# A trunk layer with RWKV-7, S5 and a gated MLP: S5's inputs without the norm's root, S5 tables by exchanged halves, one scan per batch, and masks of block products ranked first

## The chip, the cores and the metric

The kernel runs on one core of a Trainium2 chip. The metric is the device time of one execution in microseconds (us). TensorE is called PE in the profile, VectorE DVE, ScalarE ACT, GpSimd POOL, and SyncE, which issues most transfers, SP.

## The reference

One layer, 1024 tokens by 1024 channels in float32. The input projection feeds three consumers: RWKV-7 (8 heads of 64), S5 (32 groups of 16 channels with 64 complex states each), and two gates.

```python
h = rms_norm(x, norm_mix_pre)            # x * rsqrt(mean(x*x) + 1e-6) * g
proj = h @ w_in                          # [r,k,v, low-rank downs | u_s5 | gates]
o_rwkv = rwkv7_branch(p_rwkv, ...) @ w_branch_rwkv
o_s5   = s5_branch(u_s5, ...) @ w_branch_s5
mixed = (g_rwkv * o_rwkv + g_s5 * o_s5) @ w_out
x = x + rms_norm(mixed, norm_mix_post)
x = x + rms_norm(conv_ffn(rms_norm(x, norm_ffn_pre), ...), norm_ffn_post)

def s5_branch(u, ...):
    a_bar = exp(lam * dt); b_bar = ((a_bar - 1) / lam) * b
    bu = einsum('gpc,blgc->blgp', b_bar, ug)
    states = scan(s[t] = a_bar * s[t-1] + bu[t])
    y = real(einsum('gcp,blgp->blgc', c, states)) + d * ug
    y = gelu(y); return y * sigmoid(y @ w_glu + b_glu)
```

RWKV-7 scans a 64 by 64 state per head, `S = S*w + (S a) b^T + v k^T`, with decay, removal key and in-context rate made from projections of h.

## The kernel before, in words

Activations lie transposed, channels on the partitions, in 8 tiles of 128 channels and two halves of 512 tokens (th = 0 and 1). Each fp32 matmul is three: operands are split into a rounded high part (a cast, by ACT) and the rest (a subtraction, mostly DVE), and high times high (L172), low times high (L173) and high times low (L174) are summed. `hh` and `hl` are the parts of the normed input, `wh` and `wl` (for two of S5's four weight tiles `lx`) those of a weight; `gm` and `chk` are PSUM tiles.

PE's order is written out by hand. A few *lanes* hold the dependent chains (the norm, S5's tables, S5's batches, RWKV's fronts, its chain, the outputs). A list `fill` of long products (the mixing inputs `mix_in`, the gates) is laid between the steps of the lanes. A lane's `yield` names a due time T_*, in us on a clock that counts the matmuls laid down; until then fills run. The other engines' instructions are placed by a scheduler with priorities: HPN is the highest, then HPW, HP2, HP.

The start of the program: `load_x` loads x for a half; `norm` squares it, sums over channels with `sumsq` (four one-column matmuls per pair of tiles), takes the root with `rstd` (nine small DVE steps), spreads it with one matmul per 128 tokens (`spread`, L271), multiplies x by weight and root (L969) and splits. Only then does `s5_in` multiply, 4 output tiles by 2 halves by 8 input tiles by 3 matmuls, 192 in all, and ACT moves the results out of PSUM in an 8-element stride (L1075). Half 1's norm stands between these matmuls. `s5_setup` makes small 128x32 tables, after which `mix_in` and the gates fill around S5's lanes.

Per S5 batch b (8 groups), `s5_tables` makes complex products of the input and output tables (`bb`, `bw`, `bx`, `ca`, `cb`) and a cosine and a sine table of 128x8x128 (`cs`, `sn`, L569 to L578); `s5_batch` rotates the inputs (L600 to L602), scans 8 groups (L605), rotates back (L607, L608) and multiplies with PE (L613 to L615). The time step table s["rho"] holds the moduli.

In `rwkv_front` two pairs of heads (`prep_lane(0)` and `(1)`) each make their key, decay and removal-key tiles (L669 to L706), block products on PE (`cz`, L718), and a mask that DVE applies to them (L721). The outputs go through `rwkv_out` (transposes L918), a store to YR, a load, a split, and the product `mm<-t` in `merge_rk`.

Of the kernel before, what the change touches and what calls it, by code (L numbers as in the profile page):

```python
# [13 lines left out]
ALU = mybir.AluOpType  # L14
# [52 lines left out]
class Kern:  # L67
# [207 lines left out]
    def setup(self):  # L275
        nc = self.nc
        self.vecs = self.const.tile([128, NVEC], F32, name="vecs")
        self.csts = self.const.tile([128, NCST], F32, name="csts")
        nc.gpsimd.dma_start(self.csts[:, 0:128], self.a["cst"][:, 0:128])
        nc.gpsimd.dma_start(self.vecs, self.a["vec"])  # L280
        nc.gpsimd.dma_start(self.csts[:, 128:NCST], self.a["cst"][:, 128:NCST])
# [6 lines left out]

        o, n = VEC["mu"]
# [15 lines left out]
    def s5_setup(self):  # L305
# [4 lines left out]
        with self.tc.tile_pool(name="s5tmp", bufs=1) as pool:  # L310
            def sm(n=32, dt=F32):
                return pool.tile([128, n], dt, name=self.nm("sm"))
            lr, li, ls = sm(), sm(), sm()
            nc.sync.dma_start(ls, a["s5_ls"])
            nc.sync.dma_start(lr, a["s5_a"][0])
            nc.sync.dma_start(li, a["s5_a"][1])
# [173 lines left out]
    def s5_tables(self, b, d):  # L490
# [23 lines left out]
        lin(bx, bre, bc_c(s["w4"]), bim, bc_c(s["w3"]), ALU.subtract, V)  # L514
# [19 lines left out]
        ct2 = self.s5p.tile([128, 8, 9, 16], F32, tag="ct", name=self.nm("ct"))  # L534
        tab(V, cb, cre, s["q2"], 1)
        tab(V, ct2, cim, s["q1"], 1)
        V.tensor_tensor(cb[:, :, 1:9, :], cb[:, :, 1:9, :], ct2[:, :, 1:9, :], ALU.subtract)
# [27 lines left out]
        nrow = self.cst("nrow").unsqueeze(1).to_broadcast([128, 8, 128])  # L565

        def bc_n(x):
            return x[:, g8].unsqueeze(2).to_broadcast([128, 8, 128])
        V.tensor_tensor(ph, nrow, bc_n(s["fh"]), ALU.mult)  # L569
        V.tensor_scalar(cs, ph, MAGIC, -MAGIC, ALU.add, ALU.add)  # L570
        V.tensor_tensor(ph, ph, cs, ALU.subtract)
        V.tensor_tensor(sn, nrow, bc_n(s["fl"]), ALU.mult)
# [5 lines left out]
        A.activation(cs, cs, AF.Sin, bias=self.hpi, scale=-SIN_SCALE)  # L578

        d.update(ca=ca, cb=cb, cs=cs, sn=sn, toep=toep, wT=wT)  # L580
        yield 1.8, T_TRIG

    def s5_batch(self, b, d, ys):
# [4 lines left out]
        ca, cb, cs, sn, toep, wT = (d[n] for n in ("ca", "cb", "cs", "sn", "toep", "wT"))  # L588
# [3 lines left out]
        G.memset(z[:, :, 0:1], 0.0)  # L592
        rot = self.t4(shape=(128, 8, 128))
        yield 0, T_US
# [5 lines left out]
        V.tensor_tensor(rot, p1, cs, ALU.mult)  # L600
        V.tensor_tensor(r2, p2, sn, ALU.mult)
        V.tensor_tensor(rot, rot, r2, ALU.add)  # L602
        for g in range(8):
            gg = b * 8 + g
            V.tensor_tensor_scan(z[:, g, 1:128], s["rho"][:, gg:gg + 1].to_broadcast([128, 127]),  # L605
                                 rot[:, g, 0:127], 0.0, ALU.mult, ALU.add)
# [35 lines left out]
    def rwkv_front(self, d, g, th, pt, start):  # L642
# [28 lines left out]
        for e in L:  # L671
            p, tz = e["p"], e["tz"]
            V.tensor_tensor_scan(tz, self.cst("smask"), tz, 0.0, ALU.mult, ALU.add)
            A.activation(e["bk1"], c64(e["ta"]), AF.Identity, bias=self.ka_1[:, p:p + 1], scale=self.ka_h[:, p:p + 1])
            V.tensor_tensor(e["bk1"], e["bk1"], c64(e["k"]), ALU.mult)
# [6 lines left out]
        for e in L:  # L682
            y = self.small.tile([128, 8], F32, tag="sv", name=self.nm("sv"), bufs=2)
            V.tensor_scalar(y, e["st"].rearrange("p a b -> p (a b)"), 1e-24, None, ALU.max)
            V.reciprocal(y, y)
            A.copy(c64(e["yb"]), y.unsqueeze(2).to_broadcast([128, 8, 64]))
        for e in L:
            p, tz = e["p"], e["tz"]
            G.memset(e["pe"][:, :, 0:1], 1.0)
            A.activation(e["pe"][:, :, 1:65], c64(tz), AF.Exp, scale=-0.5 * CDEC)  # L690
            A.activation(tz, tz, AF.Exp, scale=0.5 * CDEC)
            A.copy(pt[:, :, p], e["pe"][:, :, 64])
            V.scalar_tensor_tensor(e["bk0"], c64(e["ta"]), 1.0, c64(e["k"]), ALU.add, ALU.mult)
            V.scalar_tensor_tensor(e["ar0"], c64(e["k"]), self.vec("k_k", p), e["pe"][:, :, 0:64], ALU.mult, ALU.mult)
            V.scalar_tensor_tensor(e["bk0"], e["bk0"], self.vec("k_k", p), c64(tz), ALU.mult, ALU.mult)
# [5 lines left out]
        for e in L:  # L701
            r, tz = e["r"], e["tz"]
            V.scalar_tensor_tensor(e["bk0"], e["bk0"], -0.5, c64(e["kb"]), ALU.mult, ALU.mult)
            V.tensor_tensor(e["ar1"], c64(r), e["pe"][:, :, 1:65], ALU.mult)
            V.tensor_tensor(c64(r), c64(r), e["bk1"], ALU.mult)
            V.tensor_tensor(e["bk1"], e["bk1"], c64(tz), ALU.mult)  # L706
            e["v"] = ld(self.RKV[8 + e["p"]])
# [3 lines left out]
        for u, e in enumerate(L):  # L711
            bk, ar = e["bk"], e["ar"]
            for q in range(2):
# [6 lines left out]
                for h in range(2):  # L720
                    V.tensor_tensor(d["gr"][:, u, 4 * q:4 * q + 4, h], ps[h], gm, ALU.mult)  # L721
# [4 lines left out]
            if u:  # L726
                for blk in range(2):
                    for h in range(2):
                        q = 64 * h + 32 * blk
                        nc.gpsimd.dma_start(d["md"][blk].rearrange("(e h) q t -> h q e t", h=2)[h],  # L730
                                            d["gr"][q:q + 32, :, :, h, 32 * blk:32 * blk + 32].rearrange("p u c t -> p (u c) t"))
            else:
# [208 lines left out]
    def load_x(self, th, pool):  # L941
        xs = []
        for k in range(NK):
            x = pool.tile([128, 512], F32, name=self.nm("x"), tag="x", bufs=16)
            self.nc.sync.dma_start(x, self.a["x"][k * 128:k * 128 + 128, th * 512:th * 512 + 512])
            xs.append(x)
        return xs

    def norm(self, th, xs, pool):

        nc = self.nc
        ss = self.chk()[:, 0:512]
        yield 0, T_X
        for k in range(0, NK, 2):
            sq = [pool.tile([128, 512], F32, tag="sq", name=self.nm("sq"), bufs=4) for _ in range(2)]
            for i in range(2):
                nc.scalar.activation(sq[i], xs[k + i], AF.Square)
            nc.vector.tensor_tensor(sq[0], sq[0], sq[1], ALU.add)
            self.sumsq(ss, sq[0], k == 0)
            yield 0.9, 1.0  # L960
        bc = self.chk()[:, 0:512]
        y = self.rstd(ss, 1e-6, 1.0 / D)
        yield 0, T_RS
        self.spread(bc, y)
        rbc = pool.tile([128, 512], F32, tag="rbc", name=self.nm("rbc"), bufs=1)
        nc.scalar.copy(rbc, bc)
        h = []
        for k in range(NK):
            nc.vector.scalar_tensor_tensor(xs[k], xs[k], self.vec("g_mix_pre", k), rbc, ALU.mult, ALU.mult)  # L969
            h.append(self.hsplit(xs[k], k, self.hp[th], eng=nc.gpsimd if k % 2 else nc.vector))  # L970
        self.h[th] = h
        yield 1.7, 5.0
# [47 lines left out]
    def rkv(self, p):  # L1020

        for mt in (4 + p, p, 8 + p):
            def use(th, ps):
# [37 lines left out]

    def s5_in(self, pool):

        w = [self.load_w(self.a["w_in"][14 + b], pool=pool if b > 1 else None) for b in range(4)]
        for th in range(2):
            h = self.h[th]
            ps = [self.gmp() for b in range(4)]
            steps = [self.mm3_steps(ps[b], w[b], 0, [x[0] for x in h], [x[1] for x in h]) for b in range(4)]
            for k in range(NK):
                for b in range(4):  # L1070
# [882 lines left out]
```

## Time and profile before

| | |
|---|---|
| Median of 3 runs | 1545.65 us (1543.03 to 1549.22) |
| The profiled execution | 1545.26 us, span 1543.5, mean granted clock 0.974 |
| PE busy | 1455.5 us (94%), 9332 matmuls |
| DVE busy | 1084.8 us (70%) |
| ACT busy | 696.9 us (45%) |
| POOL busy | 74.0 us (5%) |

The span is what the profiler recorded; 1.8 us of the execution lie around it. Busy shares are averages over stages: the start is limited by other things than the channel sub-layer. A matmul of 512 columns can take twice as long while the granted clock is low.

### The profile page before, as it was taken

Reading aid. Unit: us, or ns where it says so; the run is one execution under the profiler, and the core shown is the slowest. Engines: PE = TensorE matmul, PEld = TensorE weight load, DVE = VectorE, ACT = ScalarE, POOL = GpSimd, SP = SyncE. Lnnn points to the kernel's source line nnn. Section 1 sums busy time; section 2 is a strip of 40 time slices with the busy share of each in tenths; the row PEclk is TensorE's granted clock in tenths of the full one; section 3 lists DMA queues with packets and bytes.
Section 4 is the critical chain, followed back from the end, with each engine's and each line's share of the span. In section 5 each row is a group of like instructions: output and inputs, shape, how many; then the busy total and the mean of one; then the engine's idle time right before and its main releaser. Section 6 shows DMA issues by size and latency. Waiting matters only on the chain.

```text
span 1543.5 us, 24191 instructions
## 1 busy us (share of the span) xinstructions
PE 1455.5 (94%) x9332; PEld 1191.3 (77%) x9332; DVE 1084.8 (70%) x1783; ACT 696.9 (45%) x1077; POOL 74.0 (5%) x126
## 2 busy tenths in 40 slices
PE   5999899999999899899898999999999999999996
PEld 4788788778777677678676888788888887888785
DVE  6898784845325748466587689777777777698777
ACT  5364442533324535436444446444444444443451
POOL 2100000001100010000100000000000000000001
PEclk9999999999999899999998999999999999999998
DMA  6164242623511475424864444322222225953632
GB/s 209 42 205 126 87 127 100 206 88 117 158 57 63 152 225 161 119 79 132 269 217 153 151 144 133 111 83 82 82 82 82 82 85 195 335 169 114 214 109 109
DMA packets 130339, 210.45 MB, mean 136 GB/s; under 512 B 37696, under 2 KB 43840, under 8 KB 130224
## 3 DMA queue, kind: packets, MB, share of 16 engines
q1 hardware_dynamic: 122480, 185.17, 37.4%
q0 software_dynamic: 6592, 21.64, 4.1%
q10 hardware_dynamic: 1152, 2.10, 0.4%
q8 instruction: 73, 1.20, 0.3%
q14 instruction: 42, 0.34, 0.1%
HBM read 153.28 MB, written 53.48 MB: 134 GB/s over the span
## 4 chain that ended last, share of the span: by engine, by line
PE 76%; DVE 10%; DMA 6%; ACT 4%; issue 3%; SPq 0%; POOL 0%; ACTq 0%; DVEq 0%; POOLq 0%
PE gm L172 9%; PE gm L173 8%; PE gm L174 8%; PE rp L1384 4%; PE d L1559 4%; PE d L1558 4%; PE rp L1385 4%; PE rp L1386 4%; PE d L1560 4%; PE mm L1384 2%; PE mm L1386 2%; PE mm L1385 2%; PE ch L172 1%; PE ch L173 1%; PE ch L174 1%
## 5 line engine op out<-in xcount | busy, mean ns | idle before, releaser
L172 PE MATMUL gm<-hh,wh 128*128 128x512 f32 x688 | 282.8, 411 | 11.1 <-DVE hl L1116 5.8
L173 PE MATMUL gm<-hl,wh 128*128 128x512 f32 x688 | 271.9, 395 | 0.2 <-DVE hl L227 0.2
L174 PE MATMUL gm<-hh,wl 128*128 128x512 f32 x656 | 258.4, 394 | 0.0
L156 ACT CAST wh<-wf 128x512 fp32r<-128x512 f32 x179 | 110.8, 620 | 225.0 <-PE gm L173 138.0
L157 DVE TENSOR_TENSOR wl<-wf,wh 128x512 fp32r<-128x512 f32 x175 | 120.2, 688 | 120.6 <-ACT wh L156 112.7
L172 PEld LDWEIGHTS gm<-hh,wh 128*128 128x128 f32 x688 | 130.8, 190 | 45.1 <-DVE hl L1116 7.5
L173 PEld LDWEIGHTS gm<-hl,wh 128*128 128x128 f32 x688 | 130.9, 190 | 25.7 <-issue 1.0
L174 PEld LDWEIGHTS gm<-hh,wl 128*128 128x128 f32 x656 | 124.9, 190 | 27.3
L1559 PE MATMUL d<-xl,wh 128*128 128x512 f32 x308 | 120.8, 392 | 3.0 <-DVE xl L227 3.0
L1558 PE MATMUL d<-xh,wh 128*128 128x512 f32 x308 | 121.1, 393 | 2.4 <-ACT xh L226 2.1
L1560 PE MATMUL d<-xh,wl 128*128 128x512 f32 x308 | 120.5, 391 | 0.0
L1384 PE MATMUL rp<-t,h 128*128 128x512 f32 x216 | 84.4, 391 | 1.4 <-ACT p L1398 1.4
L1386 PE MATMUL rp<-t,l 128*128 128x512 f32 x216 | 84.2, 390 | 0.5 <-DVE l L227 0.5
L1385 PE MATMUL rp<-t,h 128*128 128x512 f32 x216 | 84.1, 389 | 0.0
L1558 PEld LDWEIGHTS d<-xh,wh 128*128 128x128 f32 x308 | 58.2, 189 | 15.9 <-ACT xh L226 2.5
L1559 PEld LDWEIGHTS d<-xl,wh 128*128 128x128 f32 x308 | 58.2, 189 | 15.8 <-DVE xl L227 3.9
L1560 PEld LDWEIGHTS d<-xh,wl 128*128 128x128 f32 x308 | 58.2, 189 | 12.3
L226 ACT CAST h<-r 128x1024 fp32r<-128x1024 f32 x34 | 35.9, 1054 | 61.1 <-PE rp L1385 32.5
L227 DVE TENSOR_TENSOR l<-r,h 128x1024 fp32r<-128x1024 f32 x34 | 41.6, 1225 | 29.2 <-ACT h L226 27.7
L1405 DVE SCALAR_TENSOR_TENSOR y<-zv,vecs,y 128x1023 f32<-128x1023 f32 (+1 forms) x36 | 46.1, 1281 | 8.5 <-ACT y L1403 8.5
L1384 PEld LDWEIGHTS rp<-t,h 128*128 128x128 f32 x216 | 40.5, 188 | 10.8 <-ACT p L1398 2.2
L1386 PEld LDWEIGHTS rp<-t,l 128*128 128x128 f32 x216 | 40.5, 188 | 9.4 <-DVE l L227 1.0
(462 smaller groups left out, 3201.3 us busy)
## 6 DMA issues: line engine op xcount, KB each, us to landing
r<-in_w_up_dram SPq DMA_DIRECT2D x36, 512.0 KB, 3.6
wf<-in_w_in_dram SPq DMA_DIRECT2D x68, 256.0 KB, 2.9
st<-in_w_down_dram SPq DMA_DIRECT2D x55, 256.0 KB, 4.2
st<-ACT SPq DMA_DIRECT2D x44, 256.0 KB, 4.8
wf<-in_w_up_dram SPq DMA_DIRECT2D x36, 256.0 KB, 2.6
ACT<-y POOLq DMA_DIRECT2D x18, 512.0 KB, 2.9
GT<-ev SPq DMA_DIRECT2D x32, 256.0 KB, 2.4
wf<-in_w_br_dram SPq DMA_DIRECT2D x32, 256.0 KB, 3.4
```

What stands on the lines that cost most here:

```text
L156: nc.scalar.copy(h[:, :n], f[:, :n])
L157: nc.vector.tensor_tensor(l[:, :n], f[:, :n], h[:, :n].bitcast(F32), ALU.subtract)
L172: mm(ps, a, xh[k], start=k == 0, stop=False)
L173: mm(ps, a, xl[k], start=False, stop=False)
L174: mm(ps, b, xh[k], start=False, stop=k == n - 1)
L1384: mm(ps, wh[:, c], xh, start=first and k == 0, stop=False, skip_group_check=True)
L1385: mm(ps, wh[:, c], xl, start=False, stop=False, skip_group_check=True)
L1386: mm(ps, wl[:, c], xh, start=False, stop=k == 3, skip_group_check=True)
L1405: V.scalar_tensor_tensor(y[:, lag:], z[:, 0:1024 - lag], self.vec(nme, i), y[:, lag:], ALU.mult, ALU.add)
L1558: mm(ps, wh[:, c], xh[:, x], start=start, stop=False, skip_group_check=True)
L1559: mm(ps, wh[:, c], xl[:, x], start=False, stop=False, skip_group_check=True)
L1560: mm(ps, wl[:, c], xh[:, x], start=False, stop=stop, skip_group_check=True)
```

## The change

- **Start.** `load_x`, `norm` and `s5_in` become one function, `start`. S5's matmuls take `gained` inputs, x times the norm's weight, without the root; DVE multiplies by the root when it moves the results out of PSUM (`evict`). Squares are summed on DVE, so that one `sumsq` per half is left. The normed input for the other products is made later by `scaled`. The weights for three S5 tiles load into the tiles of `u8`. The vectors and S5's raw inputs load on ACT's queue; the rest of the constants load last on SP's.
- **S5 tables.** `bx` and `cb` are exchanged halves of `bw` and `ca`, copied by ACT. The products with the row numbers are 16 ACT activations. Eight scans of 127 become one of 1024, whose factors are copied to `ph` and whose first column in each group is zero.
- **RWKV front.** Decay exponentials come earlier, the reciprocal norm carries the factor -0.5, products are reordered, masks of the block products are ranked under HPW, and the second pair's front begins after the first pair's masks (`grams`) and after all mixing inputs (`all_in`).
- **Numbers.** T_TAB0 20 to 44, T_BK 5 to 4, T_X gone; S5's lane has priority HP2 instead of HP.

```diff
-    def norm(self, th, xs, pool):
-        ss = self.chk()[:, 0:512]
-        yield 0, T_X
-        for k in range(0, NK, 2):
-            sq = [pool.tile([128, 512], F32, tag="sq", ...) for _ in range(2)]
-            for i in range(2):
-                nc.scalar.activation(sq[i], xs[k + i], AF.Square)
-            nc.vector.tensor_tensor(sq[0], sq[0], sq[1], ALU.add)
-            self.sumsq(ss, sq[0], k == 0)
...
-            nc.vector.scalar_tensor_tensor(xs[k], xs[k], self.vec("g_mix_pre", k), rbc, ALU.mult, ALU.mult)
-            h.append(self.hsplit(xs[k], k, self.hp[th], eng=nc.gpsimd if k % 2 else nc.vector))
...
-                self.nc.scalar.copy(y.rearrange("p i n -> p n i"), ps[b].rearrange("p (n j) -> p n j", j=8)[:, :, ::-1])
+    def start(self, pool):
...
+        def gained(th, k):
+            hi, lo = self.pair(th, k)
+            g = self.vec("g_mix_pre", k)
+            A.activation(hi, xs[th][k], AF.Identity, scale=g)
+            V.scalar_tensor_tensor(lo, xs[th][k], g, hi.bitcast(F32), ALU.mult, ALU.subtract)
+            return hi, lo
+        def square(th, k):
...
+            A.activation(sq, xs[th][k], AF.Square)
+            if k % 2:
+                V.tensor_tensor(sq, sq, last[th], ALU.add)
+                if acc[th] is not None:
+                    V.tensor_tensor(sq, sq, acc[th], ALU.add)
...
+        def scaled(th, k):
+            x = xs[th][k]
+            V.scalar_tensor_tensor(x, x, self.vec("g_mix_pre", k), rbc[th], ALU.mult, ALU.mult)
+            self.h[th][k] = self.hsplit(x, k, self.hp[th], eng=V)
+        def evict(th, b, ps):
+            y = self.ev((128, 8, 64))
+            p, r = [x.rearrange("p (n j) -> p n j", j=8)[:, :, ::-1] for x in (ps, rbc[th])]
+            V.tensor_tensor(y.rearrange("p i n -> p n i"), p, r, ALU.mult)
...
+        for th in range(2):
+            ps = [self.gmp() for b in range(4)]
+            for k in range(NK):
+                for b in range(4):
...
+                    nc.tensor.matmul(ps[b], a, hi, start=k == 0, stop=False)
+                    nc.tensor.matmul(ps[b], a, lo, start=False, stop=False)
+                    nc.tensor.matmul(ps[b], l, hi, start=False, stop=k == NK - 1)
+                    if k == NK - 1:
+                        evict(th, b, ps[b])
+                if k == (1 if th else 4):
+                    y = root(th)
+                if k == (3 if th else 6):
+                    rbc[th] = scales(th, y)
+                if th:
+                    scaled(0, k)
+                elif k >= 4:
+                    for q in (2 * k - 8, 2 * k - 7):
+                        g[1].append(gained(1, q))
+                        square(1, q)
+        for k in range(NK):
+            scaled(1, k)
...
-        lin(bx, bre, bc_c(s["w4"]), bim, bc_c(s["w3"]), ALU.subtract, V)
+        A.mul(bx[HALF[0]], bw[HALF[1]], -1.0)
+        A.copy(bx[HALF[1]], bw[HALF[0]])
...
-        tab(V, cb, cre, s["q2"], 1)
-        tab(V, ct2, cim, s["q1"], 1)
-        V.tensor_tensor(cb[:, :, 1:9, :], cb[:, :, 1:9, :], ct2[:, :, 1:9, :], ALU.subtract)
+        A.copy(cb[HALF[0], :, 1:9, :], ca[HALF[1], :, 1:9, :])
+        A.mul(cb[HALF[1], :, 1:9, :], ca[HALF[0], :, 1:9, :], -1.0)
...
-        V.tensor_tensor(ph, nrow, bc_n(s["fh"]), ALU.mult)
+        for t, f in ((ph, s["fh"]), (sn, s["fl"])):
+            for g in range(8):
+                A.activation(t[:, g], self.cst("nrow"), AF.Identity, scale=f[:, b * 8 + g:b * 8 + g + 1])
...
-        V.tensor_tensor(sn, nrow, bc_n(s["fl"]), ALU.mult)
...
+        A.copy(ph, s["rho"][:, g8].unsqueeze(2).to_broadcast([128, 8, 128]))
+        G.memset(ph[:, :, 0:1], 0.0)
...
-        for g in range(8):
-            gg = b * 8 + g
-            V.tensor_tensor_scan(z[:, g, 1:128], s["rho"][:, gg:gg + 1].to_broadcast([128, 127]),
-                                 rot[:, g, 0:127], 0.0, ALU.mult, ALU.add)
+        V.tensor_tensor_scan(*(t.rearrange("p g n -> p (g n)") for t in (z, ph, rot)), 0.0, ALU.mult, ALU.add)
...
-                for h in range(2):
-                    V.tensor_tensor(d["gr"][:, u, 4 * q:4 * q + 4, h], ps[h], gm, ALU.mult)
+                with self.tc.high_priority(HPW):
+                    for h in range(2):
+                        V.tensor_tensor(d["gr"][:, u, 4 * q:4 * q + 4, h], ps[h], gm, ALU.mult)
...
-                self.drive([(HP, self.s5_lane()), (HP, self.tab_lane())])
+                self.drive([(HP2, self.s5_lane()), (HP, self.tab_lane())])
...
-T_US, T_TAB0, T_TAB, T_TRIG, T_SCAN = 5.0, 20.0, 20.0, 12.0, 13.0
+T_US, T_TAB0, T_TAB, T_TRIG, T_SCAN = 5.0, 44.0, 20.0, 12.0, 13.0
```

PE's first instructions before. `sq` are the squares, `rsy` the root, `hh` and `hl` the high and low part of an input tile:

```order
L245 MATMUL chk_241<-ones_205,sq_242 128x1 x4
L245 MATMUL chk_241<-ones_205,sq_251 128x1 x4
L245 MATMUL chk_241<-ones_205,sq_260 128x1 x4
L245 MATMUL chk_241<-ones_205,sq_269 128x1 x4
L271 MATMUL chk_278<-csts,rsy_281 128x128 x4
L172 MATMUL gm_403<-hh_299,wh_355 128x512
L173 MATMUL gm_403<-hl_300,wh_355 128x512
```

And after, the program's first matmuls, and below the "..." the place of the one sum of squares of half 0:

```order
L1037 MATMUL gm_346<-hh_259,wh_263 128x512
L1038 MATMUL gm_346<-hl_260,wh_263 128x512
L1039 MATMUL gm_346<-hh_259,wl_264 128x512
L1037 MATMUL gm_347<-hh_259,wh_267 128x512
L1038 MATMUL gm_347<-hl_260,wh_267 128x512
...
L1039 MATMUL gm_349<-hh_302,lx_319 128x512
L245 MATMUL chk_257<-ones_192,sq_342 128x1 x4
L1037 MATMUL gm_346<-hh_324,wh_306 128x512
```

The products have moved ahead of the sum and the root; the sum stands after the fifth of eight input tiles.

DVE at the program's start before: seven small operations on the vectors, then weight splits and sums of squares (`sq`, L958):

```order
L302 TENSOR_SCALAR ka_222<-vecs 128x4
L157 TENSOR_TENSOR wl_356<-wf_357,wh_355 128x512
L157 TENSOR_TENSOR wl_362<-wf_363,wh_361 128x512
L958 TENSOR_TENSOR sq_242<-sq_242,sq_243 128x512
L958 TENSOR_TENSOR sq_251<-sq_251,sq_252 128x512
```

After, the same seven, then 18 operations of `s5_setup` (`sm`), of which the last four are shown, then the first low half of an input (`hl`, L970) and the weight splits:

```order
L335 SCALAR_TENSOR_TENSOR sm_785<-sm_783,sm_779 128x32
L330 TENSOR_TENSOR sm_901<-sm_897,sm_899 128x32
L335 SCALAR_TENSOR_TENSOR sm_787<-sm_785,sm_779 128x32
L408 RECIPROCAL sm_903<-sm_901 128x32
L970 SCALAR_TENSOR_TENSOR hl_260<-x_198,vecs,hh_259 128x512
L227 TENSOR_TENSOR wl_264<-u_0_177,wh_263 128x512
L227 TENSOR_TENSOR wl_268<-u_1_178,wh_267 128x512
```

The small S5 operations have moved from the end of the input products to ahead of the first input tile's low half.

DVE in RWKV's first front before. `gr` are the masked block products (L721), `cz` their PSUM tiles; the other rows make the second pair's tiles:

```order
L721 TENSOR_TENSOR gr_2593<-cz_2827,csts 128x4x128
L705 TENSOR_TENSOR ld_2954<-ld_2954,bk_591_2868 128x512
L721 TENSOR_TENSOR gr_2593<-cz_2828,csts 128x4x128
L706 TENSOR_TENSOR bk_591_2868<-bk_591_2868,ld_2876 128x8x64
L695 SCALAR_TENSOR_TENSOR bk_591_2868<-bk_591_2868,vecs,ld_2876 128x8x64
L157 TENSOR_TENSOR wl_3151<-wf_3152,wh_3150 128x512
L704 TENSOR_TENSOR ar_2867<-ld_2957,gr_2869 128x8x64
L693 SCALAR_TENSOR_TENSOR bk_591_2868<-ld_2882,ld_2874 128x8x64
L705 TENSOR_TENSOR ld_2957<-ld_2957,bk_591_2868 128x512
L695 SCALAR_TENSOR_TENSOR bk_591_2868<-bk_591_2868,vecs,ld_2878 128x8x64
L706 TENSOR_TENSOR bk_591_2868<-bk_591_2868,ld_2878 128x8x64
L721 TENSOR_TENSOR gr_2593<-cz_2902,csts 128x4x128
```

And after (the mask is at L719 now):

```order
L703 SCALAR_TENSOR_TENSOR bk_573_2788<-bk_573_2788,vecs,rp_2982 128x8x64
L671 SCALAR_TENSOR_TENSOR ld_3060<-csts,ld_3060 128x512
L671 SCALAR_TENSOR_TENSOR ld_3062<-csts,ld_3062 128x512
L690 SCALAR_TENSOR_TENSOR ar_3051<-ld_3056,vecs,gr_3053 128x8x64
L719 TENSOR_TENSOR gr_2789<-cz_3011,csts 128x4x128
L719 TENSOR_TENSOR gr_2789<-cz_3012,csts 128x4x128
L676 TENSOR_TENSOR bk_618_3052<-bk_618_3052,ld_3056 128x8x64
L719 TENSOR_TENSOR gr_2789<-cz_3031,csts 128x4x128
L719 TENSOR_TENSOR gr_2789<-cz_3032,csts 128x4x128
```

The masks of the first pair no longer stand among the last operations of the second pair's tiles. Elsewhere in PE's order the steps of S5's lane and of RWKV's fronts stand later among the fill matmuls: the first batch's tables after 387 large matmuls instead of 285, the first front after 906 instead of 810; between the last output transposes (half 1, L918) and the first `mm<-t` there are 106 large matmuls instead of 178.

181 lines of the change are left out of this document (99 added, 82 removed).

## The prediction

> **What bounds the kernel now.** I read the page first, then busy time by stretch, then TensorE's and the other engines' timelines at the places that the change touches.
>
> ```profile
> span 1543.5 us, 24191 instructions
> PE 76%; DVE 10%; DMA 6%; ACT 4%; issue 3%; SPq 0%; POOL 0%; ACTq 0%; DVEq 0%; POOLq 0%
> ```
>
> The profiled execution took 1545.26 us, 1543.5 of it span; the median of the runs is 1545.65, so the sum can be made against this execution. TensorE (PE) holds three quarters of the chain that ended last. The change removes almost no matmul, so what it can win is time in which PE waits or runs at a reduced clock, and what it can lose is new time of that kind. Busy time in stretches (columns: stretch, length, PE, PEld, DVE, ACT, POOL, granted clock, DMA share, GB/s) says where that time lies:
>
> ```profile
> 0.00:20.00 20.00, 7.12 (x32) 6.98 (x32) 7.07 (x18) 10.01 (x15) 2.25 (x12) 1.00 0.73 239
> 20.00:40.00 20.00, 15.46 (x65) 12.39 (x66) 17.83 (x34) 11.86 (x20) 6.45 (x4) 1.00 0.53 165
> 80.00:100.00 20.00, 20.00 (x95) 16.52 (x94) 19.42 (x36) 11.98 (x19) 0.00 (x0) 1.00 0.78 240
> 100.00:120.00 20.00, 20.00 (x99) 16.57 (x98) 19.97 (x30) 12.61 (x19) 0.00 (x0) 1.00 0.58 187
> 140.00:160.00 20.00, 18.82 (x101) 16.81 (x102) 18.67 (x28) 5.00 (x8) 0.86 (x2) 0.91 0.46 132
> 180.00:200.00 20.00, 15.93 (x83) 14.38 (x84) 17.19 (x25) 4.68 (x7) 0.11 (x1) 0.83 0.24 58
> 300.00:320.00 20.00, 14.51 (x115) 10.02 (x107) 17.51 (x30) 4.28 (x8) 2.79 (x5) 0.83 0.32 105
> ```
>
> In the first 40 us PE is busy 22.6, and much of that is sums of squares. Between 80 and 120 us PE is full, but VectorE (DVE) is too (39.4 of 40 us): work put there in the start has nowhere to go. At 140, 180 and 300 us PE has holes, and the clock sinks with them.
>
> **The start.** PE's timeline (start, duration, instruction, in brackets the idle time before it and its releaser):
>
> ```profile
> 10.92 3.55 PE L245 MATMUL chk<-ones,sq 128*128 128x1 f32 x16 [10.92 <-DVE sq L958]
> 22.06 1.12 PE L271 MATMUL chk<-csts,rsy 128*128 128x128 f32 x4 [2.52 <-DVE rsy L139]
> 25.41 0.80 PE L172 MATMUL gm<-hh,wh 128*128 128x512 f32 x1 [2.23 <-ACT hh L226]
> 28.32 0.63 PE L174 MATMUL gm<-hh,wl 128*128 128x512 f32 x1
> 28.75 0.63 PE L172 MATMUL gm<-hh,wh 128*128 128x512 f32 x1
> 36.15 0.95 PE L245 MATMUL chk<-ones,sq 128*128 128x1 f32 x8
> 77.65 0.39 PE L172 MATMUL gm<-hh,wh 128*128 128x512 f32 x1
> 79.92 0.39 PE L173 MATMUL gm<-hl,wh 128*128 128x512 f32 x1
> ```
>
> The first S5 input matmul stands at 25.41 us, because it needs the norm's root. The first row after the 192 S5 matmuls is the one at 77.65. Matmuls follow each other 0.43 us apart while PE is cold (28.32 to 28.75) and 0.227 when warm (10 steps from 77.65 to 79.92). Four sums of squares of half 1 lie between (0.95 us at 36.15); afterwards one. The 192 matmuls at 0.227 are 43.6 us, so the earliest end with a start at t is t + 43.6 + about 2 for the cold stretch.
>
> Afterwards the matmuls take x times the norm's weight, so they need neither sum nor root; those enter at eviction. What they then wait for is DVE, which makes every low half. Rows that price DVE and what feeds it:
>
> ```profile
> 7.68 0.17 DVE L291 TENSOR_SCALAR mu<-vecs 128x14 f32<-128x14 f32 x1 [7.68 <-DMA vecs<-in_vec_dram]
> 8.19 1.29 DVE L157 TENSOR_TENSOR wl<-wf,wh 128x512 fp32r<-128x512 f32 x2
> 20.26 0.16 DVE L131 TENSOR_SCALAR rsy<-rv 128x4 int32<-128x4 int32 x1
> 21.84 0.16 DVE L139 SCALAR_TENSOR_TENSOR rsy<-rsh,rsy 128x4 f32<-128x4 f32 x1
> 26.31 2.07 DVE L969 SCALAR_TENSOR_TENSOR x<-x,vecs,rbc 128x512 f32<-128x512 f32 x3
> 28.30 1.78 DVE L958 TENSOR_TENSOR sq<-sq,sq 128x512 f32<-128x512 f32 x1
> 38.98 0.18 DVE L328 TENSOR_TENSOR sm<-sm 128x32 f32<-128x32 f32 x1
> 39.09 0.18 DVE L323 TENSOR_SCALAR sm<-sm 128x32 f32<-128x32 f32 x1
> ```
>
> ```profile
> 3.60 1.25 ACT L156 CAST wh<-wf 128x512 fp32r<-128x512 f32 x2 [1.58 <-DMA wf<-in_w_in_dram]
> 76.11 1.10 ACT L1075 COPY ev<-gm 128x512 f32<-128x512 f32 x1
> ```
>
> Start to start, a 128x512 subtraction or addition costs about 0.60 us (two in 1.29), a scalar_tensor_tensor 0.66 (three in 2.07), a small 128x32 operation 0.11, and the root's steps 0.2 each.
>
> In the new DVE order the first low half stands behind 7 small operations on the vectors and 18 of s5_setup, 2.5 us. These need two loads on ACT's queue. The nearest rows: a first load on SP ended in a cast at 3.60 us, and the vectors came at 7.68 from GpSimd's queue behind another load. So the first low half starts at S = 6.1 to 10.2 us; I take 8.2, since the vectors are first in their queue now but share it with the tables' inputs. From there I follow both engines:
>
> - DVE up to the accumulated squares of half 0: 9 gained low halves at 0.66, 8 weight halves at 0.60, 7 additions at 0.60, 3 small: 15.3 us, so 23.5 us. PE, cold until about 13, takes 12 x 0.227 = 2.7 us per input tile and is through five tiles at 24.2. No wait.
> - The root of half 0 ends about 8.5 us of interleaved DVE work later, at 32.1; PE asks for it after the seventh tile, at 30.1 to 30.6: wait 1.5 to 2. Half 1 starts at about 35.9.
> - The root of half 1 by the same count at 50.4, PE there at 47.8: wait 2.6. Then four tiles, 11 us, and mix_in starts near 62.4.
>
> That is 77.65 - 62.4 = 15.3 us earlier. The bounds: S from 6.1 to 10.2 moves all of it, -2 to +2. The 8 evictions with 8-element stride are new on DVE: ACT needs 1.10 us for each, a plain DVE pass about 0.69; at the dear end 8 x 0.4 = 3 us lie on DVE, which is full. Loads: 4 MB of x and 2 MB of weights at 239 GB/s are in by 26 us, and the x tile of half 1 needed first is in by 18, so they hide, unless the two weight loads that wait for a DVE split on SP's queue hold the x tiles behind them (cost then up to 3). Together 7 to 17 us. Nothing of this start computes on GpSimd any more, so the 1.78 us instead of about 0.6 that DVE showed beside GpSimd's split (L958) goes; but the splits of odd tiles come to DVE, 8 x 0.60 = 4.8 us, which is in the count as later work.
>
> **S5's tables and batches.** Waits of PE (in all, times, longest), and groups by shape (busy, mean ns, idle before):
>
> ```profile
> PE chk L614 <- DVE t L608: 6.3, 2, 4.1
> PE chk L544 <- DVE t L600: 1.3, 1, 1.3
> PE chk L553 <- DVE t L601: 0.7, 1, 0.7
> PE cz L718 <- DVE gr L721: 5.5, 3, 4.4
> ```
>
> ```profile
> L605 DVE TENSOR_TENSOR_SCAN t<-s5rho,t 128x127 f32<-128x127 f32 x32 | 10.5, 400 | 0.1
> L569 DVE TENSOR_TENSOR t<-csts,s5fh 128x1024 f32<-128x1024 f32 x3 | 3.6, 1205 | 0.0
> L600 DVE TENSOR_TENSOR t<-chk,t 128x1024 f32<-128x1024 f32 x4 | 4.9, 1224 | 10.4 <-ACT t L578 8.8 <-PE chk L598 1.6
> L673 DVE TENSOR_TENSOR_SCAN ld<-csts,ld 128x512 f32<-128x512 f32 x4 | 4.8, 1217 | 1.4 <-DMA ld<-TZ 1.4
> L390 ACT ACTIVATE sm<-sm,hpi 128x32 f32<-128x32 f32 x2 | 0.6, 322 | 0.0
> L545 ACT COPY wT<-chk 128x1024 f32<-128x1024 f32 x3 | 3.0, 1012 | 1.1 <-PE chk L544 1.1
> ```
>
> At stake are the first three waits, 8.3 us, and the reduced clock after them: 9% of 20 us at 140 and 17% of 20 us at 180, 5.2 us; 13.5 together. The eight scans of a batch are 2.6 us (10.5 / 4), and one of 1024 by the 128x512 scan is 2 x 1.22 = 2.4: no difference. DVE loses two products with the row numbers (2.4) and three passes for cb (3.6) per batch, about 6 us. ACT gets 16 activations of 128x128: no row has this shape, the nearest (L390) is 0.32 us, so up to 5.2 us a batch; below it stands nothing that costs less than 0.2, so at least 3.2. I take 4.2, since the larger shape adds elements and the longest of the small rows is the one with a bias. The rho copy and two half copies of cb are about 1.0 each by L545. ACT is busy 5 of 20 us in the stretches at 140 and 180, so this fits; but the phase chain is 1 to 3 us longer in series, and L600 waited 8.8 us for that chain's cosine already. Against this, the first batch's tables are now asked for with a due time of 44 instead of 20, and tables come on a DVE relieved of 6 us a batch.
> The Trainium skill, page "VectorE: DVE Perf Modes", section on the TRN2 errata, speaks against this edit: SBUF operations pay a fixed cost each, a 128-element ScalarE copy measures 350 cycles, and tiles of 512 or more are advised; by its 1.2 GHz that is 0.29 us each, an estimate of 4.7 us a batch where two DVE passes took 2.4.
> I take a gain of 7 of the 13.5. The ends are 13.5 and, with the chain 2.8 longer in each of four batches and none of the 8.3 gone, -3 (8.3 less 11.2).
>
> **RWKV's first front.** The wait on the gram masks (L721), 5.5 us, and 17% of clock over 20 us, 3.4, make 8.9. The masks now stand together and ahead of ordinary work, where DVE had eight tile operations between the second and the third mask. DVE's work stays the same, and the due time before the grams is cut from 5 to 4, 6 matmuls or 1.4 us of cover. I take 3, with 0 to 7.
>
> **Cover at the merge.** S5's and RWKV's steps now stand about 100 fill matmuls later, and between the last output transposes and the first matmul on their result PE's order counts 106 large matmuls, where it had 178: 72 x 0.227 = 16.4 us less cover.
>
> ```profile
> 732.88 1.04 PE L918 MATMUL rp<-csts,mt 128*128 128x128 f32 x8
> 764.67 0.69 DVE L227 TENSOR_TENSOR t<-t,t 128x512 fp32r<-128x512 f32 x1 [2.23 <-ACT t L226]
> 782.77 0.39 PE L172 MATMUL mm<-t,wh 128*128 128x512 f32 x1
> ```
>
> Transposes end at 733.92, the first tile is split at 765.4, its matmul runs at 782.77: 17.4 us of slack, of which 1 is left. I take a loss of 2 for the later tiles; 0 to 10.
>
> **Sum.** 15.3 + 7 + 3 - 2 = 23.3 us; 1545.3 - 23.3 = 1522 us. Fills, the second half and the channel sub-layer are unchanged and cost nothing either way.
>
> **The rivals.**
> *The start gives it back.* For it: DVE is full for 100 us; with S at 10.2, dear evictions, x tiles held on SP, and the later splits late at the low-rank and first table steps, the start is worth 8, S5 2, the rest 0: 1535. Against it: each of these would have to come at its worse end.
> *The phase chain on ACT.* The 16 short activations lie in series ahead of the sine. Then S5 gives -3: 15.3 - 3 + 3 - 2 = 13.3, 1532. For it: L600's wait for ACT. Against it: 24 us more lead for the first batch. By the skill's errata section this would be the likely outcome, unless the lead hides it.
> *Slower, at the merge.* The output chain of 31.4 us (733.92 to 765.4 and its load) finds no fill at all, because fills were spent on covering S5's later start; PE idles all of it and runs cold for as much as 3.4 us of lost clock. That is 34.8 against 25.3 won: 9.5 us slower, 1555. It decides from 25 us of uncovered chain. Against it: 106 matmuls, 24 us, still stand there, so it needs the chain to stretch by as much again.
> *All waits go.* 17 + 13.5 + 7 = 37.5: 1508. For it: each hole has its DVE work reduced or ranked. Against: DVE at 100%.
> That the change does not do what it says is not open: the order has the S5 matmuls first, before any sum of squares.
>
> **How the numbers follow.** Forecast 0.52, start given back 0.15, phase chain 0.13, slower 0.07, all waits go 0.13. The range 1506 to 1539 leaves out the slower case and the far ends of the others. About 0.5% (7.7 us) is what a measurement can tell from no change: all cases but the slower one are beyond it on the fast side, with the worse end of the first rival inside it: faster 0.87, same 0.06, slower 0.07.
>
> **What would show it.** Right: the first gm matmul before 10 us, mix_in's first matmul at 60 to 65 us, waits of DVE for the roots of 1.5 and 2.6 us; L614's successor without waits over 2 us; clock 1.00 at the batches; the gram masks' wait under 3 us. Wrong: PE held by DVE's low halves in most of the first 60 us, a cosine on which the rotation waits for over 3 us in every batch, or PE idle by more than 10 us ahead of the merge's first matmul on the RWKV result.

## The result, and the profile after

The changed kernel takes 1522.48 us in the median of 4 runs (1516.56 to 1525.15), the kernel before 1547.24 beside it; the ratio is 0.9841, with a 95% interval of 0.9816 to 0.9865. The forecast was 1522. The profiled execution took 1525.15 us, 20 less than that of before.

The first lines of the page, and busy time by stretch (PE, PEld, DVE, ACT, POOL, granted clock, DMA share, GB/s):

```profile
span 1523.4 us, 24158 instructions
PE 1448.1 (95%) x9284; PEld 1180.7 (78%) x9284; DVE 1076.9 (71%) x1761; ACT 731.0 (48%) x1169; POOL 60.8 (4%) x120
```

```profile
0.00:20.00 20.00, 11.85 (x43) 9.16 (x44) 14.18 (x46) 13.10 (x23) 1.21 (x10) 1.00 0.84 273
20.00:40.00 20.00, 18.76 (x85) 14.21 (x84) 19.99 (x40) 12.45 (x23) 0.00 (x0) 1.00 0.63 173
80.00:100.00 20.00, 18.28 (x80) 14.79 (x80) 18.95 (x56) 15.10 (x26) 0.97 (x2) 1.00 0.53 185
140.00:160.00 20.00, 20.00 (x125) 17.37 (x124) 15.93 (x23) 13.94 (x31) 0.11 (x1) 1.00 0.35 106
180.00:200.00 20.00, 20.00 (x125) 17.36 (x124) 14.45 (x21) 12.11 (x26) 0.11 (x1) 1.00 0.43 127
300.00:320.00 20.00, 19.83 (x148) 16.30 (x141) 12.83 (x25) 11.99 (x29) 3.73 (x6) 1.00 0.50 147
```

The holes at 140, 180 and 300 us are closed and the clock stays at 1.00 there; between 80 and 100 us, where PE had been full, it now has a hole of 1.7 us. PE's timeline of the start:

```profile
6.79 0.80 PE L1037 MATMUL gm<-hh,wh 128*128 128x512 f32 x1 [6.79 <-ACT wh L226]
8.95 0.80 PE L1038 MATMUL gm<-hl,wh 128*128 128x512 f32 x1 [1.36 <-DVE hl L970]
24.40 1.02 PE L245 MATMUL chk<-ones,sq 128*128 128x1 f32 x8 [0.19 <-DVE sq L979]
32.06 0.65 PE L271 MATMUL chk<-csts,rsy 128*128 128x128 f32 x4 [1.04 <-DVE rsy L139]
49.77 0.65 PE L271 MATMUL chk<-csts,rsy 128*128 128x128 f32 x4 [1.71 <-DVE rsy L139]
61.80 0.47 PE L172 MATMUL gm<-hh,wh 128*128 128x512 f32 x1 [0.46 <-DVE ev L1002]
```

mix_in begins at 61.80 us instead of 77.65. Waits of PE that are new or larger (in all, times, longest):

```profile
PE mm L172 <- ACT t L226: 6.0, 2, 5.4
PE mm L173 <- DVE t L227: 4.3, 3, 2.5
PE gm L172 <- ACT ev L1096: 3.5, 3, 1.7
PE gm L173 <- DVE e L227: 3.5, 1, 3.5
```

The first two are the merge's first products on RWKV's result, the third is the low-rank step, the fourth is the product of S5's GLU for half 1 (`e` is S5's output after the gelu). No wait for S5's batches is left, and the one for the masks is 0.2 us.

To see where the 20 us arise, I take events that both kernels have. The lead at an event is how much earlier it runs, plus 0.227 us for each large matmul that has already been done in excess of before:

| event | before, us (large matmuls done) | after | lead, us |
|---|---|---|---|
| mix_in's first matmul | 77.65 (192) | 61.80 (192) | 15.9 |
| first front's norm (L680, now L681) | 282.72 (810) | 278.68 (906) | 25.8 |
| chain's inverse, half 0 (L822, now L821) | 412.82 (1239) | 397.95 (1323) | 33.9 |
| second half's front | 489.99 (1410) | 472.24 (1494) | 36.8 |
| last product of the chain, half 1 (L886, now L885) | 703.80 (1980) | 683.07 (2052) | 37.1 |
| output transposes, half 1 | 725.87 (2076) | 711.88 (2148) | 30.3 |
| first `mm<-t` | 782.77 (2280) | 751.51 (2280) | 31.3 |
| sums of squares behind the merge (L245) | 814.41 (2394) | 803.80 (2418) | 16.1 |
| last root ahead of the channel sub-layer | 904.85 (2715) | 881.39 (2715) | 23.5 |
| last root of the kernel (L271) | 1530.73 | 1510.72 | 20.0 |

So the kernel is 37 us ahead until RWKV's chain ends, loses 7 before the output transposes and 15 at the merge, gets 7 back in the output projection, and loses 3 in the channel sub-layer, which nothing changed. Runs of one kernel differ by as much as the last of these (8.6 us over four).

The 7 us ahead of the output transposes lie at S5's GLU for half 1. Its first product stands after 2088 large matmuls in both kernels, but the chain now ends after 2052 of them instead of 1980: 36 are left to cover the GLU's loads, its gelu and its splits, where there were 108. PE waits for a split, and the clock falls (busy time of the stretch after; before, PE was full between these two events at a clock of 1.00):

```profile
680.00:700.00 20.00, 16.48 (x103) 12.60 (x103) 16.95 (x43) 13.04 (x22) 0.00 (x0) 0.87 0.53 132
```

### The profile page after: what moved, and what is told of

It is laid out like the page before. It is cut to its first block, busy times and chain, and to the rows that moved or that the text cites. A ratio compares the mean times of both kernels' runs of the same rounds, so it can differ in the third digit from the quotient of the medians.

```text
span 1523.4 us, 24158 instructions
## 1 busy us (share of the span) xinstructions
PE 1448.1 (95%) x9284; PEld 1180.7 (78%) x9284; DVE 1076.9 (71%) x1761; ACT 731.0 (48%) x1169; POOL 60.8 (4%) x120
## 3 DMA queue, kind: packets, MB, share of 16 engines
q10 hardware_dynamic: 1728, 2.29, 0.4%
## 4 chain that ended last, share of the span: by engine, by line
PE 45%; DVE 8%; DMA 7%; ACT 3%; issue 2%; SPq 0%; DVEq 0%; ACTq 0%
PE rp L1445 4%; PE rp L1447 4%; PE rp L1446 4%; DMA st<-in_w_down_dram 3%; PE gm L172 2%; PE mm L1447 2%; PE mm L1445 2%; PE mm L1446 2%; PE gm L173 2%; PE ch L172 2%; PE gm L174 2%; PE ch L173 2%; PE ch L174 2%; PE mm L173 2%; PE mm L172 2%
## 5 line engine op out<-in xcount | busy, mean ns | idle before, releaser
L172 PE MATMUL gm<-hh,wh 128*128 128x512 f32 x624 | 258.1, 414 | 6.9 <-DVE hl L1177 4.6
L173 PE MATMUL gm<-hl,wh 128*128 128x512 f32 x624 | 247.0, 396 | 0.0
L174 PE MATMUL gm<-hh,wl 128*128 128x512 f32 x624 | 246.9, 396 | 0.0
L156 ACT CAST wh<-wf 128x512 fp32r<-128x512 f32 x171 | 105.8, 619 | 198.9 <-PE gm L173 110.5
L172 PEld LDWEIGHTS gm<-hh,wh 128*128 128x128 f32 x624 | 119.0, 191 | 37.6 <-DVE hl L1177 6.5
L174 PEld LDWEIGHTS gm<-hh,wl 128*128 128x128 f32 x624 | 119.0, 191 | 26.3
L173 PEld LDWEIGHTS gm<-hl,wh 128*128 128x128 f32 x624 | 119.2, 191 | 22.7 <-issue 1.0
L1620 PEld LDWEIGHTS d<-xl,wh 128*128 128x128 f32 x308 | 58.3, 189 | 16.1 <-DVE xl L227 4.2
L1619 PEld LDWEIGHTS d<-xh,wh 128*128 128x128 f32 x308 | 58.2, 189 | 15.2 <-ACT xh L226 2.4
L227 DVE TENSOR_TENSOR l<-r,h 128x1024 fp32r<-128x1024 f32 x34 | 41.7, 1225 | 30.1 <-ACT h L226 28.5
L1459 ACT COPY p<-rp 128x512 f32<-128x512 f32 x54 | 31.0, 574 | 39.5 <-PE rp L1447 39.4
```

Source lines behind the costliest of these rows:

```text
L156: nc.scalar.copy(h[:, :n], f[:, :n])
L172: mm(ps, a, xh[k], start=k == 0, stop=False)
L173: mm(ps, a, xl[k], start=False, stop=False)
L174: mm(ps, b, xh[k], start=False, stop=k == n - 1)
L1619: mm(ps, wh[:, c], xh[:, x], start=start, stop=False, skip_group_check=True)
L1620: mm(ps, wh[:, c], xl[:, x], start=False, stop=False, skip_group_check=True)
```

## The experiments

Each was timed beside the kernel before (median 1543.9 to 1544.8 in these runs, 1547.24 beside the change). The ratio is taken from all runs, so it need not be the ratio of the two medians. `no_tx` leaves a part of the result out.

| kernel | median, us | ratio to before | 95% interval |
|---|---|---|---|
| start_only | 1543.83 | 0.9997 | 0.9979 to 1.0014 |
| front_only | 1542.57 | 0.9983 | 0.9966 to 0.9999 |
| s5_only | 1538.65 | 0.9964 | 0.9947 to 0.9981 |
| start_lead | 1540.41 | 0.9957 | 0.9932 to 0.9982 |
| start_s5 | 1533.42 | 0.9936 | 0.9915 to 0.9957 |
| no_start | 1529.47 | 0.9928 | 0.9899 to 0.9957 |
| tab0_20 | 1525.02 | 0.9892 | 0.9870 to 0.9913 |
| nrow_dve | 1524.08 | 0.9870 | 0.9850 to 0.9890 |
| tab0_32 | 1524.91 | 0.9867 | 0.9839 to 0.9894 |
| masks_plain | 1523.81 | 0.9864 | 0.9833 to 0.9895 |
| t_first | 1523.61 | 0.9854 | 0.9816 to 0.9893 |
| the change | 1522.48 | 0.9841 | 0.9816 to 0.9865 |
| no_tx | 1515.84 | 0.9826 | 0.9798 to 0.9853 |

### The start alone

The diff's `setup`, `start`, `s5_setup` loads and `build` parts in the kernel before; all else old, T_TAB0 20.

> The kernel before with only the new start (S5's inputs without the root, squares added on DVE, the loads that go with it); tables, batches, fronts and due times as before. Theory (the start's gain is its own): mix_in's first matmul near 62 us instead of 77.65, S5's waits as before or a little more, cover at the merge as before; 16 us less than before, so 1531 (1528 to 1535). Rival (DVE's debt): the first batch's tables, with a due time of 20, come onto a DVE that is full to 107 us, PE waits 5 to 15 us more there, and the kernel stands at 1537 to 1546.

The start was as short as in the full change (`mix_in` from about 62 us), and the kernel was no faster at all. Waits of PE, and the stretch:

```profile
PE chk L546 <- DVE t L525: 6.8, 1, 6.8
PE chk L555 <- DVE ca L535: 6.2, 1, 6.2
```

```profile
80.00:100.00 20.00, 6.36 (x23) 4.23 (x21) 18.99 (x60) 8.22 (x12) 0.97 (x2) 0.60 0.30 104
```

PE does 6.4 us of work in 20 while DVE is busy for 19: the first tables are asked for while DVE still works off the start. Two waits of 13.1 us together, a clock of 0.60 beside them, and 1.8 us at the low-rank step use up the 15.9 us and more: at the first batch's output product the kernel stands at 141.3 us, where before stood at 138.6, and at the first front both are level (282.5 and 282.7). The rival was right.

### The start with the longer lead

```diff
-T_US, T_TAB0, T_TAB, T_TRIG, T_SCAN = 5.0, 20.0, 20.0, 12.0, 13.0
+T_US, T_TAB0, T_TAB, T_TRIG, T_SCAN = 5.0, 44.0, 20.0, 12.0, 13.0
```

> The kernel with the new start alone, and T_TAB0 44 instead of 20 in it; old tables, batches and fronts. That kernel with 20 stood where the kernel before did (1543.8 to 1544.5): its start was 16 us shorter, and PE then waited 6.8 and 6.3 us for DVE in the first batch's tables. Theory (the start's gain needs the lead, because DVE carries its work on to about 107 us): both waits go, 13 us and some clock; the later S5 steps cost up to 8 us of cover around the merge: 1532 (1528 to 1538). Rival (it is the old tables' DVE work, 6 us a batch more, that the start collides with): a wait of 5 us or more stays at the first tables, 1539 to 1545.

Both waits went, as the theory said, but only 4 to 7 us came of it: the median lies in the rival's range, though the rival's wait did not come. By the same reckoning as above the lead is 23.0 us at the first front (281.5 us, 906 matmuls) and still 20.8 at half 1's chain (632 us); at its output transposes it is 6.6 and behind the merge -3.8. The lane runs at the times of before (its front for the second half at 489.0, before 490.0), 96 matmuls later among the fills. The fills done early are then missing late, at S5's GLU for half 1 first:

```profile
700.00:720.00 20.00, 12.45 (x147) 8.84 (x146) 13.80 (x26) 12.21 (x22) 0.00 (x0) 0.87 0.48 116
```

PE was full in this stretch before. Here the shorter start only moved fills forward; the lanes did not move with it.

### S5's tables and batches alone, the front alone

Only the `s5_tables` and `s5_batch` parts (and the lane's rank); only the `rwkv_front`, `grams`, `all_in` and T_BK parts.

> The kernel before with only S5's tables and batches changed (halves copied, row products on ACT, one scan of 1024, the lane's rank); T_TAB0 stays 20, start and fronts are old. Theory (its waits go by themselves): the 8.3 us of waits at S5's batches and some clock go, the cover at the merge is as before: 1536 (1533 to 1540). Rival (the front's masks then wait for as much longer): 1542 to 1546.

> The kernel before with only RWKV's front changed: earlier exponentials, reordered products, ranked masks, the second pair's start after the first pair's masks, T_BK 4. Start, S5 tables and S5 batches are old, and the fills stand as before, so the merge has its 178 matmuls of cover. Theory (the front's gain is its own): the waits for the masks, 5.5 us, and their clock go, and something of the second half's 7 us: 1536 (1532 to 1539). Rival (the waits only move to the next step of the chain, as the start's gain alone did): 1541 to 1546.

S5's part won 5.2 us in the medians, near the upper end of the times expected: its 8.3 us of waits went, a wait of 4.4 us came at the low-rank step. The front's part won 1.3 us (2.6 by the ratio); its rival was right. The masks' wait went, and the second pair's norm waited instead (0.9 and 2.5 us), for DVE, which waited for a load of the last mixing inputs (DVE's timeline):

```profile
315.43 0.69 DVE L693 TENSOR_TENSOR ar<-ld,gr 128x512 f32<-128x512 f32 x1 [4.63 <-DMA ld<-RKV]
```

In this kernel the front starts after 810 large matmuls, beside the last tiles of `mix_in`; four of their evictions (L981) run on DVE in the 44 us from 281. In the full change it starts after 906, there are two of them in 40 us, and PE waits for nothing in the front. That the place among the fills makes this difference is borne out by the kernels with other due times. With T_TAB0 20 in the changed kernel the first front starts after 810 large matmuls again, the same two waits come back (0.9 and 3.0 us), and DVE waits for the same load:

```profile
305.08 0.69 DVE L691 TENSOR_TENSOR ar<-ld,gr 128x512 f32<-128x512 f32 x1 [5.17 <-DMA ld<-RKV]
```

From the first front to the inverse of half 0 the new front then wins 1.6 us, as it does alone (1.7). With T_TAB0 32 (after 858 matmuls) it wins 8.5, with 44 (after 906) 8.1. The old front after 906 matmuls wins 2.0 at most. No run moved the front without S5's lane.

### The start with S5, and everything but the start

> The new start with the new S5 tables and batches and T_TAB0 44; the fronts are old. With start and lead alone the time was 1540, with a wait of 6.2 us for the first front's masks and 6 us at the merge. Theory (parts add up as far as they have waits of their own): S5's last wait of 2 us goes, the masks' wait stays, 1536 (1532 to 1539). Rival (the start's 16 us comes through once S5's tables are light, and the front adds only its own 8): 1528 to 1531.

> The changed kernel with the old start: tables, batches, fronts, ranked masks and due times (T_TAB0 44) are new, the start is that of before. Theory: S5's batches lose their waits (8 us) and the first front gains about 8, and 8 of this goes back around the merge, where S5's later steps leave less cover; 9 us less than before: 1538 (1534 to 1542). If parts add up, this gain and that of the kernel with the start alone make 25. Rival (the rest is worth nothing without the start): 1545 to 1549. Rival (no loss at the merge without the start): 1528 to 1533.

Start, S5 and lead together come to 1533.4, in the theory's range; the masks' wait (4.1 us) is still there. That is 7 us less than start and lead alone in the medians (3 by the ratios). Both stand level at the first front (281.1 and 281.5 us), so it does not come from S5's batches; where it comes from stays open. Everything but the start is at 1529.5, lower than expected (1533 by the ratio). This time lies in the range of the rival without a loss at the merge, but that loss is there: PE waits 9.9 us for RWKV's tiles, as in the full change. In the two profiled executions the start is worth 9.4 us on top of it as far as the channel sub-layer: the last root ahead of it runs at 890.76 and 881.39 us, and the difference at mix_in, 17.0 us (78.78 and 61.80), has become 13.3 at the first front and 9.3 behind the merge. Over the whole executions it is 4.3 us, in the medians 7.0, by the ratios 13: the start's worth there is known no better than that.

### The lead

> The changed kernel with T_TAB0 back at 20, so that S5's steps stand about 100 matmuls earlier among the fills. Theory (lead and cover are traded): the first tables are asked for near 88 us, while DVE is full to about 107, so PE waits 6 to 15 us in the first batch; the merge has its 24 us of cover back and loses 5 to 10 us less; the time stays within 6 us of 1522. Rival (the lead is useless): no wait in the first batch, only the cover's gain, 1512 to 1516. Rival (the merge's waits do not hang on cover): the merge loses as much as now, 1530 to 1538.

> The changed kernel with T_TAB0 32, half way between 20 (1525, waits of 9.1 and 2.7 us at the first tables, none of the long ones at the merge) and 44 (1522, the other way round). Theory (lead and cover are traded one for one): 1 to 4 us of wait at the tables, the merge's waits at most half of the 10 us that they are at 44; 1520 (1516 to 1524). Rival (the merge's waits come by a step, as soon as the cover is shorter than the output chain): tables nearly free and the merge free too, 1510 to 1515.

With 20 the first tables wait again, and the merge's waits for tiles are gone. With 32 there are waits of 2.6 and 4.4 us at S5's first batch and of 2.2, 2.1 and 0.7 at the merge. All three lie within 0.5% (ratios 0.9841 to 0.9892; the intervals of 20 and 44 just miss each other): lead and cover are traded about one for one, and 32 gave no optimum between them (it came 1 us above its range). The wait at S5's GLU is part of the trade: it stands in the trace of every kernel with T_TAB0 44 (3.5 to 4.1 us on `e` L227) and in none with 20 or 32.

```profile
PE chk L545 <- DVE t L526: 9.0, 1, 9.0
```

### The short activations, and the masks' rank

```diff
-            for g in range(8):
-                A.activation(t[:, g], self.cst("nrow"), AF.Identity, scale=...)
+            V.tensor_tensor(t, nrow, bc_n(f), ALU.mult)
```

> The changed kernel with the products of row numbers and frequencies made by two DVE operations per batch again instead of 16 ACT activations (0.388 us each in the changed kernel's trace, 6.2 us a batch, against 2.4). Theory (the lead hides the chain): PE waits nowhere in S5's batches now, so nothing moves, within 4 us of 1522, or it gets worse by a few us where DVE is full. Rival (short activations are dear and lie on the path, the Trainium skill, page 'VectorE: DVE Perf Modes', section on the TRN2 errata): up to 3.8 us a batch are won, 1507 to 1515.

> The changed kernel with RWKV's masks at their old rank. Theory (the rank took the 5.5 us wait for the masks in the first front): the wait for the masks comes back by 3 to 6 us, with some clock, 1526 to 1531. Rival (the wait went because the second pair's front now starts after the first pair's masks): no wait over 1 us at the block products, 1522 within 3.

Neither moved the time. The activation costs more than I took (group by shape, mean ns):

```profile
L568 ACT ACTIVATE t<-csts,s5fl 128x128 f32<-128x128 f32 x32 | 10.0, 388 | 0.0
L604 DVE TENSOR_TENSOR_SCAN t<-t,t 128x1024 f32<-128x1024 f32 x4 | 9.1, 2286 | 0.1
...
L1002 DVE TENSOR_TENSOR ev<-gm,rbc 128x512 f32<-128x512 f32 x8 | 7.8, 1082 | 0.0
```

16 of them are 6.2 us a batch, against 4.2 taken and 2.4 for the two DVE passes that they replace. But no engine waits for them long enough to hold PE. With the masks at their old rank one wait of 0.65 us for them came back, not 3 to 6: the rank did not close the hole of 5.5 us.

### The merge

```diff
-        with self.tc.high_priority(HPW):
+        with self.tc.high_priority(HPN):
             next(merge)
```

> The changed kernel with the split of RWKV's result for the merge ranked above the weights' casts (HPN instead of HPW): the casts and splits of its four tiles stand one to four rows earlier on ACT and DVE. Theory (queue order: the third tile's cast ran at 758.69, right behind a weight's cast that had waited 4.95 us for its DMA): the waits of 5.4, 2.5 and 1.2 us shrink to under 4 together, 1515 to 1519. Rival (DMA: the load queues are full from 736 to 757 us at 370 to 415 GB/s, and PE then waits for the weight in the tile's place): the sum of the merge's waits stays within 2 us, 1522 (1519 to 1526).

```diff
-            nc.sync.dma_start(xs[k], resid(k, o))
+            if th == 0 and squares is not None:
+                nc.vector.memset(xs[k], 0.0)
+            else:
+                nc.sync.dma_start(xs[k], resid(k, o))
```

> The changed kernel without the residual's loads of half 0 (eight of 256 KB that SP issues from 738 to 767 us); DVE writes zeros to these tiles, so that the residual of half 0 is left out of the result. Ranking the merge's splits higher changed nothing (1523.6). Theory (DMA: from 736 to 757 us the engines carry 370 to 415 GB/s, and weights and tiles of the merge come late for it): the merge's waits, 10.2 us, fall under 5, 1515 (1511 to 1519). Rival (the wait is the output chain's own latency, whatever else is loaded): 1520 to 1525.

In the changed kernel the third tile's cast ran right behind a weight's cast that waited for its load (ACT's timeline, then PE's):

```profile
758.17 0.62 ACT L156 CAST wh<-wf 128x512 fp32r<-128x512 f32 x1 [4.95 <-DMA wf<-in_w_br_dram]
758.69 0.61 ACT L226 CAST t<-t 128x512 fp32r<-128x512 f32 x1
```

```profile
759.36 0.80 PE L172 MATMUL mm<-t,wh 128*128 128x512 f32 x1 [5.41 <-ACT t L226]
```

Changing the order left 8.3 us of waits and the same time: the theory of the queues' order fell. Taking 2 MB of loads out of that stretch removed the 10.2 us of waits for these tiles from the trace; other waits came, and from the output transposes to the sums behind the merge it took 87.1 us (715.97 to 803.03) instead of 91.9 (711.88 to 803.80). The median fell to 1515.84, as expected, though the intervals of the two ratios overlap, and its profiled execution (1524.33) was the longest of its five. So transfers set a part of the price of the lost cover, 4.8 us in these two profiled executions, which as a whole differ by 0.8. That the same loads fall into a shorter stretch is a reading of this, not shown by itself, and the zeros that DVE writes were not tested alone. The expectation's 370 to 415 GB/s holds from 744 us on; from 736 to 757 us the mean is 328. What sets the rest stays open.

No version beat the change with the whole computation in it.

## Why the prediction was right or wrong

The total was right to 0.5 us, and that closeness is luck: by the leads of the two profiled executions, steps that came out better than forecast make some 12 us and steps that came out worse some 15. The places and mechanisms at the start, in S5 and at the merge were right; the sizes were not. By its steps:

- **The start: right as a place, wrong as a gain.** S was forecast at 8.2 us and the first low half ran at 8.24; sum at 24.2, measured 24.40; root waits of 1.5 to 2 and 2.6, measured 1.04 and 1.71; mix_in near 62.4, measured 61.80. The evictions with the 8-element stride took 1.08 us each on DVE, the dear end. But the step that set the whole 15.3 us into the sum failed. Alone the start is worth 0.7 us (by the ratio's interval from 2 lost to 3 won), with lead 4 to 7, with everything else 4 to 13.
- **S5: right in size, in part by another way.** Forecast 7 of 13.5. All three waits went; between mix_in and S5's last product (257.30 us after 738 large matmuls, now 256.22 after 840) the lead grows by 8.4 us, low-rank waits of 3.5 us included. Alone, with T_TAB0 20, the new tables and batches are worth 5. But with the old ones and T_TAB0 44 the same stretch wins 6.4 us too (last product at 259.04 after 840), and 2.2 of the 8.3 us of waits are left: the later due time does much of what the forecast put down to the tables.
- **The front: under-sized.** Forecast 3, end 7; the lead grows by 8.1 us. Alone it is worth 1.3. The ranking, which I named as the reason, is not the cause: without it the lead still grows by 7.4. The gain comes where the front stands later among the fills. Another 3 us come in the inverse of half 0, where PE had idled for 2.8 us before and waited for no engine; the forecast has nothing there.
- **The merge: mechanism right, size too small.** Forecast 2 lost, end 10. From the first `mm<-t` to the sums behind the merge 15.2 us are lost; with what the output projection recovers, 7.8. I costed the output chain's latency at its length of before and not the transfers of that stretch. And I counted the lost cover for one chain only: S5's GLU for half 1 lost as many matmuls of cover and costs 6.8 us from the chain's end to the output transposes, where the sum has nothing. From the chain's end to the channel sub-layer 13.6 us are lost, beyond the forecast's end of 10.
- **The rival on ACT's phase chain is refuted** by the kernel with DVE's two passes. The activations took 0.388 us each here. The Trainium skill, page "VectorE: DVE Perf Modes", section on the TRN2 errata, gives 350 cycles for a ScalarE copy of 128 elements, at the 1.2 GHz that it states an estimate of 0.29 us; the trace's figure is above that. But the chain is off the path.
- **The rival "the start gives it back"** came true, but not in the full change: it is what the start does with T_TAB0 20 and the old tables. With the new tables and 20 the first tables still wait for 9.0 and 2.7 us. That the tables' due time belongs to the start, I had used only as a reason for S5's gain.

The sum treated four terms as independent. Measured alone, all with T_TAB0 20, the three parts give 0.7, 5.2 and 1.3 us, 7 together (9 by the ratios). Together with T_TAB0 20 they give 17 by the ratio (19.5 in the medians), and with 44 the whole gives 24.5 (1.59% of 1544). So they do need each other, and most of that shows without the longer lead; the longer due time adds 2.5 us in the medians and 8 by the ratios, shifts S5 and the front among the fills, and the steps at the end pay for the shift. Which pair of parts makes the surplus was not separated: no run has two of the three with T_TAB0 20.

## What to carry to other kernels

In a program that hides chains of dependent steps behind a fixed stock of filling work, an earlier start of the fills is no gain by itself: follow the lane's own times to the end of the stock, and ask what is uncovered there, at every chain that stands there and not only at the longest. Cost the parts together, since a full engine carries its debt to the next step that asks for it. Where cover shrinks, count the bytes that must now land in it, beside the latency of the chain.

## What the hardware showed that I had not expected

- A 128x128 ACT activation took 0.388 us, longer than the 128x32 ones (0.21 to 0.32) suggested; a DVE eviction of 128x512 with an 8-element stride took 1.08 us, as much as ACT's (1.10).
- One 1024-long scan took 2.29 us, less than two of 512 (2.43).
- In the stretch of 20 us with two waits of PE, 13 us together, the mean granted clock was 0.60.
- Executions of one kernel spread by 2 to 15 us here (start_lead from 1528.9 to 1543.8), so that a single profiled one decides no question of 5 us about the total.
